# A decoder layer in fp32r products: eight plain half products for the first two MLP-down pairs, squares of x added on VectorE

## The chip, the cores and the metric

The kernel runs on one NeuronCore of a Trainium2 chip. The metric is the device time of one execution in microseconds (us). PE is TensorE (matmuls), DVE is VectorE, ACT is ScalarE, POOL is GpSimd and SP is SyncE, which issues DMAs.

## The reference, cut to what matters

One layer of a hybrid decoder on x of 512 tokens by 2048 features, all in float32. What the change touches are the sum of squares of the first norm, the norm of q and k, and the last product:

```python
def rms_norm(x, g):
    y = xf * lax.rsqrt(jnp.mean(xf * xf, axis=-1, keepdims=True) + EPS)
    return (y * g.astype(jnp.float32)).astype(x.dtype)
...
        xn = rms_norm(x, norm_mix_g[l])
        proj = xn @ w_in[l]
...
    q = rms_norm(q.reshape(b, s, ATTN_HEADS, HEAD_DIM), q_g)
    k = rms_norm(k.reshape(b, s, ATTN_HEADS, HEAD_DIM), k_g)
...
        x = x + merged @ w_out[l]
        h = rms_norm(x, norm_mlp_g[l]) @ w_mlp_up[l]
        x = x + jnp.square(jax.nn.relu(h)) @ w_mlp_down[l]
```

The hidden width of the MLP is 8192; attention has 8 heads of 64.

## The kernel before

Everything is held transposed: features on the 128 partitions, the 512 tokens along the free axis. A float32 product is made of three fp32r matmuls (`mm3`, L173): each factor is split into a rounded high part, cast on ACT, and a low part, the difference, made on DVE; hi x hi, hi x lo and lo x hi are added in PSUM. Names end in h and l for the parts (`x4h`, `x4l`, `wh`, `wl`).

**Front** (L245 to L266). A loop over the 16 feature tiles of x loads a tile, splits it with the norm's weight (`split`: ACT L221, DVE L222), splits the weights that belong to it (`fill`, L150 and L151, four k at a time), and multiplies it into `pq` and `pk`, the first q and k projection. ACT squares each tile (L227) and POOL adds it to `acc` (L229). Then `pv`, the values, begins with a weight piece of 1040 columns. `token_scale` turns `acc` into the norm's factor of each token while `pv` runs: its two PE steps come after the waits (3, 6). For ACT and DVE the instruction order of this part is set by the language's scheduler, for PE by the code.

**Chains.** Norms and attention run as generators that yield a time: `clock` adds up PE time by a formula as matmuls are issued, `poll` goes on with a chain whose time has come, and `finish` runs a chain to its end, setting the clock ahead where it must. `pair(i)` projects q and k of two heads (`proj`), normalises them (`qk_norm`: squares, `q3ms` on PE, a square root, a reciprocal, a split into `q3nh` and `q3nl`), and attends block by block: logits `pl`, softmax on DVE and ACT, transposition `pt` on PE, its copy `pT` on ACT (L472), and `po` on PE. Pairs 1 to 3 run beside the projections of the short convolutions (`pgc`, `pxx` and others).

**MLP.** From the gates on, PE, ACT and DVE follow one order written by the program. A product of a 256 x 256-block matrix by a matrix is done as seven products of halves instead of eight (Strassen's scheme in Winograd's form, products 1 to 7 in the order 1, 6, 7, 4, 5, 2, 3). That takes sums of quarters of the left factor (weights, `zd`, L671, made on DVE) and of the right (token sums, L858 to L861), and sums of the results (L933). An item is one or two left operands: DMA, sums, cast (L713), low part (L719); `step` prepares items two or three ahead of the one that PE multiplies, in left buffers of which there are three. What else DVE and ACT have to do waits in a list, `later`: `wait_for` puts a task in with a time, and a mark "must" for those that are taken at the next step whether or not there is room; `flush` takes tasks out by time alone until a right factor is there.

The right factors of MLP down are d0 to d38. Each is fetched by a POOL DMA (`std`, L909), cast (`shd`, L886) and made low (`sld`, L890), 1792 columns each. `h30` and `h31` are the last two outputs of MLP up: they are scaled (L1276), squared (L1284), get their token sums, and go to HBM, from where their factors are fetched again. The first two pairs of MLP down (`run_duo` with `down_first`) run together with K in two parts, so that they begin with d0 to d3 (part 0) and go on with d4 to d8 (part 1); seven PSUM banks hold both pairs. From pair 2 on, `run_pair` has eight factors a pair, into `pda` to `pdd`.

These lines put the factors of part 1 in the list and start the duo:

```python
    TIMES = (0, 2.5, 11, 13)
...
    renew((4, 5, 6, 7), TIMES, (6, 7, 8, 9))
    run_duo(
        down_first,
```

Of the kernel before, what the change touches and what calls it, by code (L numbers as in the profile page):

```python
# [11 lines left out]
ALU = mybir.AluOpType  # L12
# [86 lines left out]
def body(nc, tc, ctx, dram):  # L99
# [97 lines left out]
    def chain(steps):  # L197
        c = [steps, None]
        chains.append(c)
        advance(c)  # L200
        return c
# [23 lines left out]
    def add_square(acc, src, tag, name, eng):  # L225
        sq = acc if name.endswith("_0") else t512(tag, f"sq{name}")
        A.activation(sq, src, AF.Square)  # L227
        if sq is not acc:
            eng.tensor_tensor(out=acc, in0=acc, in1=sq, op=ALU.add)  # L229
# [12 lines left out]

    xg = []  # L245
    acc = t512("y", "acc1")
    pq, pk = bank("pq0", "aux"), bank("pk0", "aux")
    w0 = {}
    for k in range(KT):
        h, r = divmod(k, 8)  # L250
        if r == 0:
            w0 = {c: load(2 * h + e) for e, c in enumerate((XQ, XK))}
        raw = t512("m", f"xr{k}")
        for c in (XQ, XK):
            if r % 4 == 0:
                fill(*w0[c], slice(r * P, (r + 4) * P))
            if c == XQ and k == 0:
                nc.sync.dma_start(gm, dram["par"][:, :KT])
            if c == XQ:
                nc.sync.dma_start(raw, dram["xT"][k])  # L260
        xg.append(split(raw, "a", f"x{k}", gm[:, k : k + 1]))
        for c, ps in ((XQ, pq), (XK, pk)):
            mm3(ps, [p[:, r * P : (r + 1) * P] for p in w0[c][1:3]], xg[k], k == 0, k == KT - 1)
        add_square(acc, raw, "y", f"1_{k}", G)

    used[0] = len(weights)  # L266

    ident = const("ident", [P, P])
    rcnt = const("rcnt", [P, 16])
# [78 lines left out]
    def qk_norm(src, g, name):  # L348
        sq = t512("y", f"{name}sq")
        A.activation(sq, src, AF.Square)  # L350
        hi, lo = split(sq, "y", f"{name}q")
        yield 10
        ms = bank(f"{name}ms", "aux")
        mm(ms, eblk, hi, True, False)
        mm(ms, eblk, lo, False, True)
        v, s = t512("y", f"{name}v"), t512("y", f"{name}s")
        V.tensor_scalar(v, ms, EPS, None, ALU.add)
        inv_sqrt(sq, v, v, s)
        V.scalar_tensor_tensor(out=src, in0=src, scalar=g, in1=sq, op0=ALU.mult, op1=ALU.mult)
        qk[name] = split(src, "m", f"{name}n")  # L360

    def log1p_exp_neg_abs(z, mk, name):
# [33 lines left out]
    ncd = hbm.tile([8, S], F32, name="ncd")  # L396

    def first_pair():
        yield from token_scale(acc, "r1", n1)
        first.extend((proj(XQ, "q0", pq), proj(XK, "k0", pk)))  # L400

    def forget(z):
# [80 lines left out]

    def pair(i):
        q = proj(XQ + i * P, f"q{i}")
        qc = chain(qk_norm(q, qg8, f"q{i}"))
        k = proj(XK + i * P, f"k{i}")
        finish(qc)

        def steps():  # L490
            yield from qk_norm(k, pc("kg"), f"k{i}")
            yield 12
            yield from attend(i)

        chain(steps())
# [121 lines left out]
    class Phase:  # L617

        def __init__(self, kind, a, b, ks):
            self.kind, self.a, self.b, self.ks = kind, a, b, ks
            self.w = len(ks) * P
            self.raws, self.sums = {}, {}

# [8 lines left out]
        def quarter(self, q):  # L634
# [18 lines left out]
            o = 512 * (q % 2) if two else 0  # L653
            return self.raws[key][:, o : o + self.w]

        def room(self, n):

            two = self.w <= 512
            if n == 1 or not two:
                self.z = lz[0][1].tile([P, 1024], F32, name=f"z{self.kind}{self.a}_{n}", tag="z", bufs=2)  # L660
            o = 512 * (n - 1) if two else 0
            return self.z[:, o : o + self.w]

        def sums_of(self, i):
# [12 lines left out]

            def s2():
                x = a11()
                sums[2] = self.room(2)  # L680
                tt(sums[2], sums[1], x, ALU.subtract)

            return {
                1: [s1], 6: [s2], 7: [lambda: tt(a21(), a11(), a21(), ALU.subtract)],
                3: [lambda: tt(sums[2], a12(), sums[2], ALU.subtract)],
            }.get(i, [])

        def source(self, i):
            if i in (5, 6, 3):
                return self.sums[1 if i == 5 else 2]  # L690
            return self.quarter({1: 0, 7: 1, 4: 2, 2: 3}[i])

        def groups(self):
            return ((1, 6), (7, 4), (5, 2), (3,)) if self.w <= 512 else tuple((i,) for i in ORDER)

    class Item:
# [9 lines left out]
        def cast(self):  # L706
            self.hi, self.lo = (
                pool.tile([P, 1024], F32R, name=f"u{q}{self.name}", tag=f"w{q}", bufs=3) for q in "hl"
            )
            self.left = {}  # L710
            for n, i in enumerate(self.group):
                sl = slice(512 * n, 512 * n + self.phase.w)
                A.copy(self.hi[:, sl], self.phase.source(i))  # L713
                self.left[i] = (self.hi[:, sl], self.lo[:, sl])

        def sub(self):
            for i, (hi, lo) in self.left.items():
                spend(self.phase.w)
                V.tensor_tensor(out=lo, in0=self.phase.source(i), in1=f(hi), op=ALU.subtract)  # L719
# [73 lines left out]
    def flush(until=lambda: False):  # L793
        settle()
        while later and not until():
            pop(min(later, key=lambda t: t[0]))

    def result(name, where, tag, cols):

# [31 lines left out]
    def window(n, m):  # L831

        return [(J % UP, ("d", J)) for J in range(n, m)]

    def duo(kind, pairs, parts):

        return [[planned(Phase(kind, *pair, part)) for pair, part in zip(pairs, ps)] for ps in parts]

    def whole(kind, a, b, ks):
        return planned(Phase(kind, a, b, ks))  # L840
# [7 lines left out]
    up_first = duo("u", [(0, 0), (1, 0)], [[eight("u")[:4]] * 2, [eight("u")[4:]] * 2])  # L848
    up_pairs = [whole("u", n, 0, eight("u")) for n in range(2, UP - 2)]
    up_last = duo("u", [(UP - 2, 0), (UP - 1, 0)], [[eight("u")[:4]] * 2, [eight("u")[4:]] * 2])  # L850
    down_first = duo("d", [(0, 0), (1, 0)], [[window(0, 4), window(1, 4)], [window(4, 8), window(4, 9)]])
    down_pairs = [whole("d", n, 0, window(n, n + 8)) for n in range(2, UP)]

    def token_sums(t):
# [60 lines left out]
    def half_wide(name, where):  # L915
        return wide(name, where, "u", 1, S)

    def product(phase, i, left, ps, first, last, more):

        for n, (_, key) in enumerate(phase.ks):  # L920
            if key not in right:
                flush(lambda: key in right)
            wk = [t[:, n * P : (n + 1) * P] for t in left[i]]
            xk = [t[:, AT[i] * H : (AT[i] + 1) * H] for t in right[key]]
            mm3(ps, wk, xk, first and n == 0, last and n == len(phase.ks) - 1, more)
            poll()

# [3 lines left out]
    def add(out, ps, x):  # L931
        spend(H)
        V.tensor_tensor(out=out, in0=ps, in1=x, op=ALU.add)  # L933

    turn = [0]

# [240 lines left out]
    def residual(n, ps):  # L1177

        j, e = n % 8, n // 8
        r = t512("r", f"x1_{n}")  # L1180
        G.dma_start(r, dram["xT"][n])

        def first():
            spend(S)
            add_in(r, ps, r)
            G.dma_start(x1d[j][:, e * S : (e + 1) * S], r)
            wait_for(scaled, S, 0, n == 15)
            wait_for(square)

        def square():  # L1190
            sq = acc if n == 0 else t512("g", f"sq{n}")
            A.activation(sq, r, AF.Square)
            if n:
                wait_for(lambda: add_in(acc, acc, sq), S)

        def scaled():
            if e == 0:
                factors[j] = wide(f"x2_{j}", *((st1, "st1", 1) if j % 2 else (opool, "o", 1)))
            o = factors[j]
            V.scalar_tensor_tensor(  # L1200
                out=o[:, e * S : (e + 1) * S], in0=r, scalar=pc("g_mlp", n), in1=p, op0=ALU.mult, op1=ALU.mult,
            )
# [12 lines left out]

        return [first]
# [106 lines left out]
    def put(n, r):  # L1323
# [4 lines left out]
                nc.sync.dma_start(dram["out"][q + 8 * e], x1d[q][:, e * S : (e + 1) * S])  # L1328

    renew((4, 5, 6, 7), TIMES, (6, 7, 8, 9))  # L1330
    run_duo(
        down_first,
        [lambda n=n: (result(f"y{n}", upool[0], "o", 7 * H)[:, R], half_wide(f"ud{n}", upool[0])) for n in range(2)],
        lambda: renew((8, 9), (1, 9), (10, UP + 7)),
# [105 lines left out]
```

## Time and profile before

| | |
|---|---|
| time, 3 runs | 2760.41, 2760.54 (median), 2760.94 us |
| the profiled execution | 2758.59 us; its span 2756.7, mean granted clock 0.995 |
| PE busy | 2709.0 us, 98% of the span, 19904 matmuls |
| DVE busy | 2163.2 us, 78% |
| ACT busy | 1229.9 us, 45% |
| POOL busy | 180.8 us, 7% |

The profile is of one execution. Its span runs from the first instruction to the last; 1.89 us of the execution's time lie around it. A row's start is in us from the span's start. In a timeline, "[3.39 <-DVE x4l L222]" says that the engine was idle for 3.39 us before the row and that the write of `x4l` on DVE ended that. The start-to-start time of two instructions can be shorter than the duration shown, because they overlap in an engine's pipeline. The granted clock is a share of the full 2.4 GHz.

### The profile page before, as it was taken

The numbers are of one execution on the slowest core, as the hardware profiler recorded it, in microseconds if no ns is written. First come the engines' busy times: TensorE is split into PE (matmuls) and PEld (weight loads), VectorE is DVE, ScalarE is ACT, GpSimd is POOL, SyncE is SP. The second block draws the span as 40 slices with busy tenths as digits, with TensorE's granted clock in tenths as the row PEclk, the third lists the DMA queues.
The fourth block names the chain that finished last, engine by engine and source line by source line (L and its number), as shares of the span: only waits on it lengthen the run. The fifth ranks groups of instructions, "written<-read, shape, count | busy, mean of one in ns | idle before, by whom it ended". The sixth has DMA issues, their size and how long they took to land. (4 is left out here: it accounts for less than half of the span.)

```text
span 2756.7 us, 48177 instructions
## 1 busy us (share of the span) xinstructions
PE 2709.0 (98%) x19904; PEld 2540.5 (92%) x19904; DVE 2163.2 (78%) x2664; ACT 1229.9 (45%) x1520; POOL 180.8 (7%) x298
## 2 busy tenths in 40 slices
PE   8999999999999999999998999999997999999999
PEld 7787777789999999998888999999997999999999
DVE  6875655476889888887548988888888888888887
ACT  5443334454444444443224444444444544444443
POOL 3000000000000000003110000000000000000000
PEclk9999999999999999999999999999999999999999
DMA  5222223564444444447453444544446666656575
GB/s 178 94 98 80 84 77 103 182 229 161 143 158 141 139 145 156 143 146 252 144 177 120 174 165 144 164 144 165 144 146 210 185 186 173 189 170 190 170 206 155
DMA packets 143901, 429.49 MB, mean 156 GB/s; under 512 B 16696, under 2 KB 30904, under 8 KB 143680
## 3 DMA queue, kind: packets, MB, share of 16 engines
q1 hardware_dynamic: 101536, 279.19, 30.0%
q0 software_dynamic: 32496, 129.65, 16.2%
q10 hardware_dynamic: 9648, 17.57, 1.7%
q8 instruction: 156, 2.56, 0.4%
q14 instruction: 65, 0.53, 0.1%
HBM read 350.04 MB, written 79.97 MB: 156 GB/s over the span
## 5 line engine op out<-in xcount | busy, mean ns | idle before, releaser
L713 ACT CAST uhd<-wqd 128x1024 fp32r<-128x1024 f32 (+3 forms) x136 | 135.6, 999 | 216.8 <-PE pdd L173 80.8
L713 ACT CAST uhg<-wqg 128x1024 fp32r<-128x1024 f32 (+1 forms) x136 | 135.6, 999 | 185.3 <-PE pgd L173 96.4
L713 ACT CAST uhu<-wqu 128x1024 fp32r<-128x1024 f32 (+1 forms) x144 | 136.2, 951 | 159.8 <-PE pud L173 86.7
L719 DVE TENSOR_TENSOR uld<-wqd,uhd 128x1024 fp32r<-128x1024 f32 (+3 forms) x136 | 157.1, 1158 | 55.0 <-ACT uhd L713 55.0
L151 DVE TENSOR_TENSOR wl<-wr,wh 128x1024 fp32r<-128x1024 f32 (+2 forms) x100 | 121.6, 1218 | 90.1 <-ACT wh L150 86.1
L719 DVE TENSOR_TENSOR ulg<-wqg,uhg 128x1024 fp32r<-128x1024 f32 (+1 forms) x136 | 157.1, 1158 | 33.5 <-ACT uhg L713 33.5
L150 ACT CAST wh<-wr 128x1024 fp32r<-128x1024 f32 (+2 forms) x100 | 101.1, 1014 | 159.9 <-PE pb L173 32.2
L713 ACT CAST uhg<-zg 128x1024 fp32r<-128x1024 f32 (+1 forms) x102 | 102.0, 1000 | 150.0 <-DVE ulg L719 103.3
L719 DVE TENSOR_TENSOR ulu<-wqu,uhu 128x1024 fp32r<-128x1024 f32 (+1 forms) x144 | 157.7, 1100 | 7.4 <-ACT uhu L713 7.3
L713 ACT CAST uhu<-zu 128x1024 fp32r<-128x1024 f32 (+1 forms) x108 | 103.1, 955 | 125.3 <-DVE ulu L719 70.7
L713 ACT CAST uhd<-zd 128x1024 fp32r<-128x1024 f32 (+3 forms) x102 | 102.0, 1000 | 125.3 <-PE pdb L173 55.7
L173 PE MATMUL pda<-shd,uld 128*128 128x256 f32 x480 | 134.8, 281 | 1.1 <-DVE uld L719 1.1
L173 PE MATMUL pda<-sld,uhd 128*128 128x256 f32 x480 | 134.5, 280 | 0.0
L173 PE MATMUL pda<-shd,uhd 128*128 128x256 f32 x480 | 134.5, 280 | 0.0
L173 PE MATMUL pdd<-shd,uld 128*128 128x256 f32 x480 | 134.5, 280 | 0.0
L173 PE MATMUL pdb<-shd,uld 128*128 128x256 f32 x480 | 134.5, 280 | 0.0
L173 PE MATMUL pdb<-shd,uhd 128*128 128x256 f32 x480 | 134.5, 280 | 0.0
L173 PE MATMUL pdd<-shd,uhd 128*128 128x256 f32 x480 | 134.4, 280 | 0.0
L173 PE MATMUL pdd<-sld,uhd 128*128 128x256 f32 x480 | 134.4, 280 | 0.0
L173 PE MATMUL pdb<-sld,uhd 128*128 128x256 f32 x480 | 134.4, 280 | 0.0
L173 PE MATMUL pgb<-shg,ulg 128*128 128x256 f32 x480 | 134.2, 280 | 0.0
L173 PE MATMUL pgd<-shg,ulg 128*128 128x256 f32 x480 | 134.2, 280 | 0.0
(1462 smaller groups left out, 10455.2 us busy)
## 6 DMA issues: line engine op xcount, KB each, us to landing
wqg<-in_w SPq DMA_DIRECT2D x120, 512.0 KB, 3.5
wqu<-in_w SPq DMA_DIRECT2D x112, 512.0 KB, 3.5
wr<-in_w SPq DMA_DIRECT2D x84, 512.0 KB, 3.5
std<-zd POOLq DMA_DIRECT2D x39, 896.0 KB, 5.0
zd<-h POOLq DMA_DIRECT2D x32, 896.0 KB, 4.8
bk<-b ACTq DMA_DIRECT2D x64, 256.0 KB, 2.6
b<-bk POOLq DMA_DIRECT2D x32, 512.0 KB, 4.6
wo<-in_w SPq DMA_DIRECT2D x32, 512.0 KB, 3.6
```

The source lines that it names most:

```text
L150: A.copy(hi, raw)
L151: V.tensor_tensor(out=lo, in0=raw, in1=f(hi), op=ALU.subtract)
L173: T.matmul(out, w, x, start=start, stop=stop, skip_group_check=more)
L713: A.copy(self.hi[:, sl], self.phase.source(i))
L719: V.tensor_tensor(out=lo, in0=self.phase.source(i), in1=f(hi), op=ALU.subtract)
```

## The change

Six edits. (1) The squares of x are added on DVE; the additions are written behind the loop and the scheduler places them. (2) `first_pair` waits (10, 6) instead of (3, 6) in `token_scale`. (3) `qk_norm` yields 5 more before the split, and `pair` no longer finishes q's chain before it goes on. (4) The first two pairs of MLP down are eight plain products of halves: each quarter of the weights times its half of the tokens, no left sums; p0 and p1 hold the parts that are added into both rows, q and r the others, six PSUM banks in all. The first quarters are cast two at a time, 1024 wide. (5) `flush` takes tasks marked "must" first. (6) Among the residuals of the layer's first half, the scaling of both n = 7 and n = 15 is marked "must".

```diff
-        add_square(acc, raw, "y", f"1_{k}", G)
+        raws.append(raw)

     used[0] = len(weights)
+    for k, raw in enumerate(raws):
+        add_square(acc, raw, "y", f"1_{k}", V)
...
         V.scalar_tensor_tensor(out=src, in0=src, scalar=g, in1=sq, op0=ALU.mult, op1=ALU.mult)
+        yield 5
         qk[name] = split(src, "m", f"{name}n")
...
-        yield from token_scale(acc, "r1", n1)
+        yield from token_scale(acc, "r1", n1, (10, 6))
...
         q = proj(XQ + i * P, f"q{i}")
-        qc = chain(qk_norm(q, qg8, f"q{i}"))
+        chain(qk_norm(q, qg8, f"q{i}"))
         k = proj(XK + i * P, f"k{i}")
-        finish(qc)
...
         def groups(self):
+            if self.plain:
+                return ((0, 1), (2, 3)) if self.w <= 512 else ((0,), (1,), (2,), (3,))
...
         while later and not until():
-            pop(min(later, key=lambda t: t[0]))
+            pop(min(later, key=lambda t: (not t[4], t[0])))
...
+    PLAIN = {0: (("p0", 1), ("r0", 5)), 1: (("p1", 1), ("r1", 5)), 2: (("q1", 2), ("r1", 3)), 3: (("q0", 2), ("r0", 3))}
+
+    def run_plain_duo(phases, outs, between, after):
...
+                def products(item):
+                    then = []
+                    for i in item.group:
+                        for b, at in PLAIN[i]:
+                            p = ps[b][:, x * H : (x + 1) * H]
+                            opens = part == 0 and x == 0 and (b[0] != "r" or i < 2)
+                            closes = part == 1 and x == 1 and (b[0] != "r" or i > 1)
+                            product(phase, i, item.left, p, opens, closes, True, at)
+                            if part == 0 or b[0] == "r" and i < 2:
+                                continue
+                            if b[0] == "p":
+                                then.append(lambda p=p, u=(u2, u3)[i]: A.copy(u, p))
+                            else:
+                                c = {"q0": c11, "r0": c12, "q1": c21, "r1": c22}[b]
+                                then.append(lambda c=c, p=p, u=(u2, u3)[int(b[1])]: add(c, p, u))
+                    return then
...
-            wait_for(scaled, S, 0, n == 15)
+            wait_for(scaled, S, 0, j == 7)
...
     renew((4, 5, 6, 7), TIMES, (6, 7, 8, 9))
-    run_duo(
+    run_plain_duo(
         down_first,
```

Three places show the new orders. The first is DVE at the end of the front. The last `wl` of 1040 columns here belongs to the values `pv`; `eblk` is a constant. Before:

```order
L222 SCALAR_TENSOR_TENSOR x12l<-xr_295,gm,x12h 128x512
L346 TENSOR_SCALAR qg_372<-par 128x1
L518 TENSOR_SCALAR sp_689<-par 128x4
L222 SCALAR_TENSOR_TENSOR x13l<-xr_316,gm,x13h 128x512
L222 SCALAR_TENSOR_TENSOR x14l<-xr_331,gm,x14h 128x512
L276 MEMSET eblkf 128x128
L222 SCALAR_TENSOR_TENSOR x15l<-xr_346,gm,x15h 128x512
L278 MEMSET eblkf 64x64 x2
L279 CAST eblk<-eblkf 128x128
L151 TENSOR_TENSOR wl_386<-wr_384,wh_385 128x1040
L368 TENSOR_SCALAR lama<-lama 128x4
```

After:

```order
L229 TENSOR_TENSOR acc_83<-acc_83,sq_10_343 128x512
L278 MEMSET eblkf 128x128
L229 TENSOR_TENSOR acc_83<-acc_83,sq_11_346 128x512
L280 MEMSET eblkf 64x64
L229 TENSOR_TENSOR acc_83<-acc_83,sq_12_349 128x512
L280 MEMSET eblkf 64x64
L229 TENSOR_TENSOR acc_83<-acc_83,sq_13_352 128x512
L281 CAST eblk<-eblkf 128x128
L229 TENSOR_TENSOR acc_83<-acc_83,sq_14_355 128x512
L348 TENSOR_SCALAR qg_372<-par 128x1
L151 TENSOR_TENSOR wl_386<-wr_384,wh_385 128x1040
L229 TENSOR_TENSOR acc_83<-acc_83,sq_15_358 128x512
```

The additions stand between the low parts of x and ahead of `wl_386`; one, of tile 15, stands behind it.

The second is ACT at pair 3 of attention (`l,st` is the softmax, `wh` weights of the gates, `yd` the output of attention). Before:

```order
L288 ACT_TABLE_LOAD
L288 ACTIVATE q3s<-q3v 128x512
L150 CAST wh_3224<-wr_3223 128x1024
L350 ACTIVATE k3sq<-k_3214 128x512
L218 CAST k3qh<-k3sq 128x512
L150 CAST wh_3273<-wr_3272 128x1024
L218 CAST q3nh<-q_3098 128x512
L472 COPY pT_3255<-pt_3252 128x256
L482 COPY yd_2846<-po_3184 128x128
L453 ACT_TABLE_LOAD
```

After:

```order
L456 ACT_TABLE_LOAD
L456 ACTIVATE l_3186,st_3191<-l_3186,st_3191 128x384
L475 COPY pT_3199<-pt_3196 128x256
L150 CAST wh_3217<-wr_3216 128x1024
L352 ACTIVATE k3sq<-k_3207 128x512
L218 CAST k3qh<-k3sq 128x512
L150 CAST wh_3254<-wr_3253 128x1024
L218 CAST q3nh<-q_3068 128x512
L475 COPY pT_3288<-pt_3285 128x256
L456 ACTIVATE l_3275,st_3280<-l_3275,st_3280 128x384
L150 CAST wh_3320<-wr_3319 128x1024
```

`q3nh` still stands right ahead of a `pT`; a softmax block and another `pT` now stand between the square root of q (`q3s`) and `q3nh`.

The third is the beginning of MLP down: DVE around `sld` of d6 and d7, then ACT around `shd` of the same factors (`h_21287` is h30, `h_21425` is h31). DVE before; `sld` of d6 stands six rows above this piece:

```order
L861 TENSOR_TENSOR h_21287<-h_21287 128x256
L671 TENSOR_TENSOR zd_1_21737<-wqd_0_2_21734,zd_1_21737 128x512
L719 TENSOR_TENSOR uld_5_21817<-zd_1_21737,uhd_5_21816 128x512
L719 TENSOR_TENSOR uld_5_21817<-wqd_0_2_21734,uhd_5_21816 128x512
L1276 SCALAR_TENSOR_TENSOR h_21425<-h_21425,ups 128x512 x2
L858 TENSOR_TENSOR h_21425<-h_21425 128x256
L859 TENSOR_TENSOR h_21425<-h_21425 128x256
L860 TENSOR_TENSOR h_21425<-h_21425 128x256
L861 TENSOR_TENSOR h_21425<-h_21425 128x256
L890 TENSOR_TENSOR sld_21795<-std_21655,shd_21794 128x1792
```

DVE after; both low parts, of d6 and d7, are at its end:

```order
L1338 SCALAR_TENSOR_TENSOR h_21425<-h_21425,ups 128x512
L741 TENSOR_TENSOR uld_2_21632<-wqd_0_2_21633,uhd_2_21631 128x384 x2
L912 TENSOR_TENSOR sld_21642<-std_21474,shd_21641 128x1792
L1338 SCALAR_TENSOR_TENSOR h_21425<-h_21425,ups 128x512
L737 TENSOR_TENSOR uld_0_21696<-wqd_0_0_21697,uhd_0_21695 128x1024
L737 TENSOR_TENSOR uld_2_21743<-wqd_0_2_21744,uhd_2_21742 128x1024
L880 TENSOR_TENSOR h_21425<-h_21425 128x256
L881 TENSOR_TENSOR h_21425<-h_21425 128x256
L882 TENSOR_TENSOR h_21425<-h_21425 128x256
L883 TENSOR_TENSOR h_21425<-h_21425 128x256
L912 TENSOR_TENSOR sld_21749<-std_21639,shd_21748 128x1792
L912 TENSOR_TENSOR sld_21752<-std_21702,shd_21751 128x1792
```

ACT before:

```order
L713 CAST uhd_1_21759<-wqd_0_1_21731 128x512
L713 CAST uhd_1_21759<-zd_1_21737 128x512
L886 CAST shd_21763<-std_21611 128x1792
L713 CAST uhd_7_21787<-wqd_0_1_21731 128x512
L713 CAST uhd_7_21787<-wqd_0_2_21734 128x512
L886 CAST shd_21794<-std_21655 128x1792
L1284 ACTIVATE h_21287<-h_21287 128x1024
L713 CAST uhd_5_21816<-zd_1_21737 128x512
L713 CAST uhd_5_21816<-wqd_0_2_21734 128x512
L1284 ACTIVATE h_21425<-h_21425 128x1024
```

ACT after:

```order
L725 CAST uhd_0_21695<-wqd_0_0_21697 128x1024
L725 CAST uhd_2_21742<-wqd_0_2_21744 128x1024
L908 CAST shd_21748<-std_21639 128x1792
L908 CAST shd_21751<-std_21702 128x1792
L1346 ACTIVATE h_21425<-h_21425 128x1024
L731 CAST uhd_0_21799<-wqd_0_0_21801 128x640
L731 CAST uhd_1_21860<-wqd_0_1_21862 128x640
```

On DVE the left sums are gone and the token sums of h31 stand ahead of both low parts instead of between them; on ACT the square of h31 stands behind both casts, with the two casts of part 1's first left operands ahead of them.

## Rows read from the trace of the kernel before

**Rows 1.** The page: busy time and share of the span of each engine, and instructions.

```profile
PE 2709.0 (98%) x19904; PEld 2540.5 (92%) x19904; DVE 2163.2 (78%) x2664; ACT 1229.9 (45%) x1520; POOL 180.8 (7%) x298
```

**Rows 2.** The waits of PE, grouped by who waits for what: total us, times, longest.

```profile
PE pd L173 <- DVE sld L890: 11.1, 2, 10.3
PE pu L173 <- DVE ulu L719: 9.9, 5, 4.0
...
PE po L173 <- ACT pT L472: 4.6, 2, 3.5
PE pq L173 <- DVE x4l L222: 3.4, 1, 3.4
PE pq L173 <- DVE x12l L222: 3.3, 1, 3.3
```

**Rows 3.** Busy time in stretches of the span: stretch, its length, then busy us (and instructions) of PE, weight loads, DVE, ACT and POOL, the granted clock of PE, the busy share of the DMA engines, GB/s. The first three lie in the front, the fourth behind the wait for `pT` at pair 3, the last two at the beginning of MLP down.

```profile
8.30:21.40 13.10, 9.71 (x33) 7.37 (x33) 12.71 (x9) 10.01 (x18) 12.55 (x8) 0.87 1.06 393
21.50:24.30 2.80, 2.80 (x14) 2.25 (x13) 2.80 (x5) 1.27 (x3) 0.00 (x0) 1.00 0.39 158
24.40:35.90 11.50, 8.19 (x31) 6.21 (x31) 11.19 (x10) 10.38 (x19) 11.03 (x7) 0.90 0.31 93
...
409.40:415.80 6.40, 6.34 (x17) 4.87 (x18) 1.62 (x4) 2.26 (x5) 0.03 (x1) 0.50 0.01 4
...
2132.90:2136.30 3.40, 3.33 (x16) 3.34 (x17) 0.01 (x1) 0.10 (x1) 0.53 (x1) 0.52 0.93 316
...
2140.00:2158.00 18.00, 16.69 (x136) 15.91 (x134) 16.65 (x24) 7.22 (x10) 1.42 (x2) 1.00 0.68 198
```

**Rows 4.** The timeline of POOL in the front: start, busy us, instruction, count.

```profile
8.28 13.16 POOL L229 TENSOR_TENSOR acc<-acc,sq 128x512 f32<-128x512 f32 x8 [7.83 <-ACT sq L227]
24.33 11.62 POOL L229 TENSOR_TENSOR acc<-acc,sq 128x512 f32<-128x512 f32 x7 [2.89 <-ACT sq L227]
```

**Rows 5.** The timeline of DVE in the front.

```profile
7.71 0.75 DVE L222 SCALAR_TENSOR_TENSOR x1l<-xr,gm,x1h 128x512 fp32r<-128x512 f32 x1
...
15.17 1.76 DVE L222 SCALAR_TENSOR_TENSOR x4l<-xr,gm,x4h 128x512 fp32r<-128x512 f32 x1
...
22.52 0.74 DVE L222 SCALAR_TENSOR_TENSOR x8l<-xr,gm,x8h 128x512 fp32r<-128x512 f32 x1
23.18 0.74 DVE L222 SCALAR_TENSOR_TENSOR x9l<-xr,gm,x9h 128x512 fp32r<-128x512 f32 x1
```

**Rows 6.** The timeline of PE in the front.

```profile
13.20 0.39 PE L173 MATMUL pq<-x4h,wh 128*128 128x512 f32 x1
...
20.96 0.39 PE L173 MATMUL pq<-x6h,wh 128*128 128x512 f32 x1
...
29.36 0.39 PE L173 MATMUL pq<-x12h,wh 128*128 128x512 f32 x1
...
40.16 0.28 PE L173 MATMUL pv<-wl,x0h 128*128 128x260 f32 x1
```

**Rows 7.** The timelines of PE and ACT at pair 3 of attention, and of ACT at pair 2.

```profile
395.01 0.50 PE L173 MATMUL q3ms<-q3qh,eblk 128*128 128x512 f32 x1
...
408.51 0.62 ACT L218 CAST q3nh<-q 128x512 fp32r<-128x512 f32 x1 [3.14 <-DVE q L359]
409.04 0.37 ACT L472 COPY pT<-pt 128x256 f32<-128x256 f32 x1
...
409.46 1.12 PE L173 MATMUL po<-pT,val 128*64 128x128 f32 x4 [3.54 <-ACT pT L472]
...
335.18 0.62 ACT L218 CAST q2nh<-q 128x512 fp32r<-128x512 f32 x1 [2.22 <-DVE q L359]
336.26 0.37 ACT L472 COPY pT<-pt 128x256 f32<-128x256 f32 x1 [0.46 <-PE pt L179]
```

**Rows 8.** The timelines of PE and, for the last two rows, of ACT at the beginning of MLP down.

```profile
2100.88 0.41 PE L173 MATMUL pd<-shd,uhd 128*128 128x256 f32 x1
...
2118.06 0.28 PE L173 MATMUL pd<-shd,uld 128*128 128x256 f32 x1
...
2120.04 0.28 PE L173 MATMUL pd<-sld,uhd 128*128 128x256 f32 x1
...
2132.97 0.58 PE L173 MATMUL pd<-sld,uhd 128*128 128x256 f32 x1 [10.28 <-DVE sld L890]
...
2158.93 0.39 PE L173 MATMUL pda<-shd,uld 128*128 128x256 f32 x1 [0.91 <-DVE uld L719]
...
2120.57 1.68 ACT L886 CAST shd<-std 128x1792 fp32r<-128x1792 f32 x1
...
2128.09 1.06 ACT L1284 ACTIVATE h<-h 128x1024 f32<-128x1024 f32 x1 [3.85 <-DVE h L1276]
```

**Rows 9.** The timeline of DVE at the beginning of MLP down.

```profile
2096.51 0.68 DVE L671 TENSOR_TENSOR zd<-wqd,wqd 128x512 f32<-128x512 f32 x1
2097.23 0.69 DVE L671 TENSOR_TENSOR zd<-zd,wqd 128x512 f32<-128x512 f32 x1
2097.84 0.68 DVE L719 TENSOR_TENSOR ulu<-zu,uhu 128x512 fp32r<-128x512 f32 x1
...
2129.18 0.42 DVE L858 TENSOR_TENSOR h<-h 128x256 f32<-128x256 f32 x1 [1.12 <-ACT h L1284]
...
2130.89 2.02 DVE L890 TENSOR_TENSOR sld<-std,shd 128x1792 fp32r<-128x1792 f32 x1
```

More of the change, by code (lines that the diff above doesn't have):

```diff
@@ L241, in pc @@
         return par[:rows, c : c + 1]
-    xg = []
+    xg, raws = [], []
     acc = t512("y", "acc1")
@@ L617, in body, with __init__ @@
     class Phase:
-        def __init__(self, kind, a, b, ks):
-            self.kind, self.a, self.b, self.ks = kind, a, b, ks
+        def __init__(self, kind, a, b, ks, plain=False):
+            self.kind, self.a, self.b, self.ks, self.plain = kind, a, b, ks, plain
             self.w = len(ks) * P
@@ L654, in quarter, with raw @@
             return self.raws[key][:, o : o + self.w]
+        def raw(self, q):
+            self.quarter(q)
+            return self.raws[q // 2]
         def room(self, n):
@@ L664, in sums_of @@
         def sums_of(self, i):
+            if self.plain:
+                return []
             a11, a21, a22, a12 = (lambda q=q: self.quarter(q) for q in range(4))
@@ L688, in source @@
         def source(self, i):
+            if self.plain:
+                return self.quarter(i)
             if i in (5, 6, 3):
@@ L693, in groups @@
         def groups(self):
+            if self.plain:
+                return ((0, 1), (2, 3)) if self.w <= 512 else ((0,), (1,), (2,), (3,))
             return ((1, 6), (7, 4), (5, 2), (3,)) if self.w <= 512 else tuple((i,) for i in ORDER)
@@ L710, in cast @@
             self.left = {}
+            if self.phase.plain and self.phase.w == 512:
+                A.copy(self.hi, self.phase.raw(self.group[0]))
+                for n, i in enumerate(self.group):
+                    self.left[i] = [t[:, 512 * n : 512 * (n + 1)] for t in (self.hi, self.lo)]
+                return
             for n, i in enumerate(self.group):
@@ L716, in sub @@
         def sub(self):
+            if self.phase.plain and self.phase.w == 512:
+                spend(1024)
+                V.tensor_tensor(out=self.lo, in0=self.phase.raw(self.group[0]), in1=f(self.hi), op=ALU.subtract)
+                return
             for i, (hi, lo) in self.left.items():
@@ L833, in window, with duo @@
         return [(J % UP, ("d", J)) for J in range(n, m)]
-    def duo(kind, pairs, parts):
-        return [[planned(Phase(kind, *pair, part)) for pair, part in zip(pairs, ps)] for ps in parts]
+    def duo(kind, pairs, parts, plain=False):
+        return [[planned(Phase(kind, *pair, part, plain)) for pair, part in zip(pairs, ps)] for ps in parts]
     def whole(kind, a, b, ks):
@@ L850, in body @@
     up_last = duo("u", [(UP - 2, 0), (UP - 1, 0)], [[eight("u")[:4]] * 2, [eight("u")[4:]] * 2])
[L851 removed]
+    down_first = duo("d", [(0, 0), (1, 0)], [[window(0, 4), window(1, 4)], [window(4, 8), window(4, 9)]], True)
     down_pairs = [whole("d", n, 0, window(n, n + 8)) for n in range(2, UP)]
@@ L916, in half_wide, with product @@
         return wide(name, where, "u", 1, S)
-    def product(phase, i, left, ps, first, last, more):
+    def product(phase, i, left, ps, first, last, more, at=None):
         for n, (_, key) in enumerate(phase.ks):
@@ L923, in product @@
             wk = [t[:, n * P : (n + 1) * P] for t in left[i]]
-            xk = [t[:, AT[i] * H : (AT[i] + 1) * H] for t in right[key]]
+            c = AT[i if at is None else at] * H
+            xk = [t[:, c : c + H] for t in right[key]]
             mm3(ps, wk, xk, first and n == 0, last and n == len(phase.ks) - 1, more)
@@ L933, in add @@
         V.tensor_tensor(out=out, in0=ps, in1=x, op=ALU.add)
+    PLAIN = {0: (("p0", 1), ("r0", 5)), 1: (("p1", 1), ("r1", 5)), 2: (("q1", 2), ("r1", 3)), 3: (("q0", 2), ("r0", 3))}
+    def run_plain_duo(phases, outs, between, after):
+        turn[0] += 2
+        sums = ("p0", "r0", "p1", "r1", "q1", "q0")
+        ps = {i: bank(f"p{phases[0][0].kind}{i}", "mm" if n < 4 else "aux") for n, i in enumerate(sums)}
+        for part in range(2):
+            if part:
+                between()
+            for x in range(2):
+                phase = phases[part][x]
+                if part:
+                    out, u = outs[x]()
+                    c11, c12, c21, c22, u2, u3 = blocks(out, u)
+                def products(item):
[14 more added lines that the diff above has]
+                    return then
+                for _ in phase.groups():
+                    step(products)
+                if part:
+                    after[x](out)
     turn = [0]
```

## Prediction

> **What bounds the kernel now.** I read the engine totals first. TensorE (PE) is busy 98% of the span, the next engine 78% [rows 1], so time leaves only where PE waits, where it runs at its lower clock, or where its instructions are fewer. Next the waits of PE [rows 2]: five groups hold most of its idle time. Two, `pq` for `x4l` (3.4 us) and for `x12l` (3.3), lie in the front; `po` for `pT` (4.6, longest 3.5) in attention; `pu` for `ulu` (9.9, longest 4.0) and `pd` for `sld` (11.1, longest 10.3) where MLP up turns into MLP down. A long wait also costs afterwards: right behind these waits the granted clock is 0.50 to 0.52, that is 1.2 GHz, for 3 to 6 us, while it is 1.00 elsewhere, also over 18 us near the end of the first two down pairs in which PE idles 1.31 us in short waits (16.69 busy of 18.00) [rows 3].
>
> **Front.** In the loop over the 16 tiles of x, POOL adds the squares: 8 adds in 13.16 us and 7 in 11.62, 1.65 us each [rows 4]. While it does, one x-low of VectorE (DVE) takes 1.76 us; before POOL starts and in the pause between the two runs it takes 0.74 to 0.75 [rows 5]. The DMA share doesn't go with it: it is 1.06 in the first run, but 0.31 in the second, where x-lows are as slow, and 0.39 in the pause [rows 3]. So I take POOL's adds as the cause.
>
> The change takes the 15 adds from POOL and gives DVE 15 of 128x512. Their price beside a quiet POOL is not in this trace; the bounds are 0.60 us (about the start-to-start time from `zd` to `ulu`, both of 512 columns, 2097.23 to 2097.84 [rows 9]) and 1.76 (the slow x-low). I take 0.60, since that is a DVE add with POOL not adding, and for x-lows 0.66 (22.52 to 23.18 [rows 5]). Walking DVE and ACT in the new order with these, `x4l` is ready at about 12.2 and `x12l` at 22.9. PE, no longer stopped, takes 8.40/6 = 1.40 us for one k (six tiles from 20.96 to 29.36 [rows 6]) and comes to them at 13.4 and 24.6. Both waits go, and the slow clock behind them. The loop, from 13.20 on, ends at 13.20 + 12 x 1.40 = 30.0.
>
> What is late next is the first low weight for the values, `wl` of 1040 columns: it stands behind `x15l` and five of the adds, starts at 30.15 and ends at 31.4. PE's second `pv` matmul, at 40.16 now [rows 6], then comes at 31.4, after a wait of 1.3 us: **-8.75 us**. Were the adds 0.1 us dearer, the fourteen ahead of `wl` would give back 1.4.
>
> [...]
>
> Waits (10, 6) instead of (3, 6) for the token scale let PE work on for 7 us before the ones matmuls want the accumulator; the last add ends at about 32, early enough. I count 0.
>
> **Attention.** At pair 3, ACT casts `q3nh` at 408.51, when `q` is ready at last, and copies `pT` only behind it; PE waits 3.54 us for that and then runs at the low clock [rows 7]. The granted clock is 0.50 from there to 415.8 [rows 3], and half of the 5 us of 512-column matmuls in it, 2.5, is lost: this stall costs 3.54 + 2.5 = 6.0. The order on ACT stays, `q3nh` and then `pT` (ACT rows of the change's section); what moves is PE. The finish that is dropped had set the planner's clock ahead of PE's work, so that `po` came early in PE's order: it is wanted 10.9 us after `q3ms` (395.01 to 405.9) and `pT` ready 14.4 after [rows 7]. In the new order 17.7 us of PE's work lie between, and by my walk of DVE and ACT `pT` is ready 14.6 after `q3ms`. That wait goes, with 3 us to spare. At pair 2, `q2nh` stands ahead of a `pT` in both orders, at 335.18 and 336.26 now, without a wait of PE [rows 7]; in the new order it is an earlier `pT`, which PE wants 1.2 us before it is there, too short for the clock. Sum **-4.8**, bounds -6.0 (no new wait) and 0 (the stall moves to pair 2 at its old price).
>
> **The first two pairs of MLP down.** Eight products of halves instead of seven: 16 factors x 8 x 3 = 384 matmuls of 256 columns, not 336. At the full clock they start 0.117 us apart (17 steps from 2118.06 to 2120.04 [rows 8]), so 48 x 0.117 = **+5.6** on PE, the busy engine. In return DVE loses all left sums (four a phase, 16 in all; the two of 512 columns shown start 0.72 and 0.61 before what follows [rows 9], so about 10 us), and its casts, subtractions and result adds are fewer.
>
> What that is worth lies in one wait. `sld7` starts at 2130.89 and PE resumes at 2132.97 [rows 8, 9]; it stands on DVE behind the left sums, the scaling and squaring of h31 and the token sums of h31 (2129.18). The new order, by the same durations: before the transition, `h30` scaled (0.6) takes the place of two left sums (1.3) ahead of `ulu`, so PE starts down at 2100.15 instead of 2100.88. Part 0 is then 168 matmuls, 19.7 us and 0.6 at the low clock: 2120.5; the six of part 1 that have their factors bring it to 2121.2. On ACT the second cast of part 1 waits for a left buffer that PE frees after 132 matmuls, at 2116.3; behind it stand `shd6`, `shd7` (1.69 long) and the squaring of h31 (1.06) [rows 8], which ends at 2121.7. DVE's token sums of h31 follow, 2121.7 to 2123.5, then `sld6` to 2125.5 and `sld7` (2.02 long) to 2127.45. So PE waits 4.2 and 1.3 us and resumes at 2127.47, 5.5 us earlier than now, with 206 matmuls of the first two pairs left instead of 179.
>
> I compare at the third matmul of pair 2, at 2158.93 after a wait of 0.91 [rows 8]. From the resumption to it are 181 matmuls and 25.96 us: 21.2 of matmuls, 1.31 of short waits for left factors, 0.91, 1.63 for the low clock (0.48 of 3.40 [rows 3]) and 0.9 that I can't place. In the new order the left factors stand ahead of the result adds, so the short waits and the 0.91 go: 208 x 0.117 + 1.63 + 0.9 = 26.9, at 2154.4. **-4.6**. Bounds: -10.28 - 1.63 - 1.31 - 0.91 + 5.6 = -8.5 (every wait gone), and +5.6 (nothing gained).
>
> "Must first" in flush, and the last residual of up scaled at j = 7: at most one 512-column add in another place, 0.6; I take 0.
>
> **Sum.** -8.75 - 4.8 - 4.6 = -18.15. On the profiled execution (2758.59) this gives 2740.4. The runs shown have a median 1.95 above that execution, so I say **2742**.
>
> **Rivals.**
> (a) The transition gives nothing: the wait at `sld7` keeps its 10 us because ACT's chain (buffer, `shd7`, square) or the transfer of d7 comes later than I walked. For it: five ACT steps hang on one freed buffer, and the new left casts are 1024 wide. Against: DVE loses some 10 us of work there. Then -13.5 + 0 to +5.6: 2747 to 2753. Chance 0.17.
> (b) The front gives back part: `wl` comes later, because an add costs a full 0.69 or waits for its square on ACT. For it: 1.3 us of wait is already forecast, the chain of adds is dependent, and dependent sums start 0.72 apart (2096.51 to 2097.23 [rows 9]). 15 x 0.1 to 0.2 = 1.5 to 3: 2744 to 2745. Chance 0.12. It lies in the forecast's own range.
> (c) Attention's stall only moves to pair 2, and the transition gives nothing: -8.75 + 5.6 = -3.2: 2757, no change. Chance 0.04.
> (d) Slower: the slow x-lows are not POOL's doing but that of ACT's traffic in the same stretch (ACT is busy 10.0 of the 13.1 us [rows 3]). Then the 14 adds ahead of `wl` cost 1.7 each on a DVE that is already full: 23.5 us later there, with the 8.75 not gained, +23.5 - 4.8 - 4.6 = +14: 2775. It decides from 9.4/14 = 0.7 us per add on. Against: in the pause of POOL, with ACT still busy 1.27 of 2.80 us, the x-low falls at once to 0.74 [rows 3, 5]. Chance 0.04.
> (e) More than forecast, both late waits gone: 2733 to 2737. Chance 0.08.
> Forecast itself: 0.55, its own range 2737 to 2747.
>
> **Numbers.** The range 2733 to 2753 takes in (a), (b) and (e) nearly whole; outside are (c), (d) and what I have not seen, some 0.15. No change, within 0.2%, is 2755.0 to 2766.1 (0.2% is 5.5 us, about what a measurement of this kernel can tell). Faster: 0.55 + 0.17 + 0.12 + 0.08 = 0.92; same 0.04; slower 0.04.
>
> **What will show it.** Front: x-lows all near 0.75 us, no PE wait for `x4l` or `x12l`, `pv` at about 31 with a wait of 1 us for `wl`. If x-lows stay at 1.76, (d) holds. Attention: no wait of over 3 us for `pT`, clock 1.00 where it was 0.50. Transition: h31's token sums ahead of both `sld6` and `sld7`, PE's longest `pd` wait about 4 us, with a second of 1.3, and the third matmul of pair 2 at 2154.4 - 13.55 = 2140.8. A longest wait of over 8 us means (a).

## The result and the profile after

The changed kernel takes 2745.34 us (median of 4 runs, 2743.41 to 2747.65) where the kernel before takes 2760.74 (4 runs, 2760.41 to 2761.14): a ratio of 0.9945, with a 95% interval of 0.993 to 0.996. The forecast was 2742, in a range of 2733 to 2753. The direction and the range held; the gain is 15.4 us where 18.2 to 18.7 were forecast, and it is made up otherwise than I said.

The profiled execution took 2745.49 us, its span is 2743.7 against 2756.7. Its waits of PE, which answer to [rows 2] (who waits for what, total us, times, longest):

```profile
PE pu L173 <- DVE ulu L741: 9.7, 6, 3.3
PE pq L173 <- ACT x0h L221: 6.8, 1, 6.8
PE pdp L173 <- DVE sld L912: 5.0, 2, 3.9
PE pb L173 <- DVE y10l L219: 1.3, 1, 1.3
PE po L173 <- ACT pT L475: 1.2, 2, 1.0
PE pv L173 <- DVE wl L151: 1.2, 1, 1.2
PE pb L173 <- ACT y10h L218: 1.1, 1, 1.1
```

The waits for `x4l`, for `x12l` and the long one for `pT` are gone, and that for `sld` fell from 11.1 to 5.0. New are 1.2 us for `wl`, which was forecast, and two waits of `pb` for `y10`, the first factor of the second branch, which were not. The very first wait, for the first tile of x, is 6.8 us long instead of 5.4: its DMA landed later, and the code up to it is the same.

The front on DVE, to be held against [rows 5] (timeline: start, us, instruction):

```profile
12.28 0.74 DVE L222 SCALAR_TENSOR_TENSOR x4l<-xr,gm,x4h 128x512 fp32r<-128x512 f32 x1
...
23.70 0.74 DVE L222 SCALAR_TENSOR_TENSOR x12l<-xr,gm,x12h 128x512 fp32r<-128x512 f32 x1
24.37 0.68 DVE L229 TENSOR_TENSOR acc<-acc,sq 128x512 f32<-128x512 f32 x1
24.97 0.75 DVE L222 SCALAR_TENSOR_TENSOR x13l<-xr,gm,x13h 128x512 fp32r<-128x512 f32 x1
...
31.98 1.23 DVE L151 TENSOR_TENSOR wl<-wr,wh 128x1040 fp32r<-128x1040 f32 x1
```

and on PE, against [rows 6]:

```profile
6.84 0.79 PE L173 MATMUL pq<-x0h,wh 128*128 128x512 f32 x1 [6.84 <-ACT x0h L221]
...
33.27 0.39 PE L173 MATMUL pv<-wl,x0h 128*128 128x260 f32 x1 [1.17 <-DVE wl L151]
```

All x-lows take 0.74 to 0.75 us, an addition starts 0.60 before what follows (24.37 to 24.97), and from PE's first matmul to the second of `pv` it is 33.27 - 6.84 = 26.43 us, where it was 40.16 - 5.39 = 34.77.

The beginning of MLP down, against [rows 8, 9]. DVE, then ACT, then PE:

```profile
2113.95 0.42 DVE L880 TENSOR_TENSOR h<-h 128x256 f32<-128x256 f32 x1 [2.91 <-ACT h L1346]
...
2115.68 3.95 DVE L912 TENSOR_TENSOR sld<-std,shd 128x1792 fp32r<-128x1792 f32 x2
...
2109.69 3.27 ACT L908 CAST shd<-std 128x1792 fp32r<-128x1792 f32 x2
2112.87 1.05 ACT L1346 ACTIVATE h<-h 128x1024 f32<-128x1024 f32 x1
...
2117.75 0.44 PE L173 MATMUL pdp<-sld,uhd 128*128 128x256 f32 x1 [3.88 <-DVE sld L912]
2119.68 0.58 PE L173 MATMUL pdp<-sld,uhd 128*128 128x256 f32 x1 [1.07 <-DVE sld L912]
...
2146.50 0.28 PE L173 MATMUL pda<-shd,uld 128*128 128x256 f32 x1
```

DVE waits 2.91 us for the square of h31, then does its token sums and then both low parts back to back; that is the order forecast, and PE's two waits for it are 3.88 and 1.07 long (4.2 and 1.3 forecast).

Where the time went, read at four PE instructions that both traces have: at the second `pv` matmul the changed kernel is 6.89 us ahead (40.16 to 33.27), 8.34 of it from the loop, less 1.45 for the later first tile. At a matmul late in MLP up it is 7.76 ahead (2085.92 to 2078.16), so attention and all that follows it have brought 0.9. At the third matmul of pair 2 of MLP down it is 12.43 ahead (2158.93 to 2146.50): 4.67 from the transition. At the end of the span it is 13.0.

### The profile page after: what moved, and what is told of

Read it like the earlier page. It is cut to its first block, busy times and chain, and to the rows that moved or that the text cites. A ratio compares the mean times of both kernels' runs of the same rounds, so it can differ in the third digit from the quotient of the medians.

```text
span 2743.7 us, 48190 instructions
## 1 busy us (share of the span) xinstructions
PE 2711.5 (99%) x19952; PEld 2544.5 (93%) x19952; DVE 2137.7 (78%) x2641; ACT 1223.0 (45%) x1506; POOL 156.5 (6%) x283
## 5 line engine op out<-in xcount | busy, mean ns | idle before, releaser
L731 ACT CAST uhd<-wqd 128x1024 fp32r<-128x1024 f32 (+2 forms) x128 | 130.8, 1024 | 230.3 <-PE pdd L173 86.8
L741 DVE TENSOR_TENSOR uld<-wqd,uhd 128x1024 fp32r<-128x1024 f32 (+2 forms) x128 | 151.8, 1187 | 69.6 <-ACT uhd L731 69.6
L731 ACT CAST uhd<-zd 128x1024 fp32r<-128x1024 f32 x90 | 94.5, 1050 | 105.7 <-PE pdb L173 55.7
```

## The experiments

**The lost gain of attention.** In the trace after, at the point where PE goes over to the second branch (PE, then ACT):

```profile
489.49 0.57 PE L173 MATMUL pb<-y10h,wh 128*128 128x512 f32 x1 [1.14 <-ACT y10h L218]
491.32 0.80 PE L173 MATMUL pb<-y10l,wh 128*128 128x512 f32 x1 [1.26 <-DVE y10l L219]
491.91 0.63 PE L173 MATMUL pb<-y10h,wl 128*128 128x512 f32 x1
492.34 0.63 PE L173 MATMUL pb<-y11h,wh 128*128 128x512 f32 x1
...
488.38 0.48 ACT L475 COPY pT<-pt 128x384 f32<-128x384 f32 x1
...
488.81 0.62 ACT L218 CAST y10h<-w 128x512 fp32r<-128x512 f32 x1
```

`y10h` stands on ACT behind a `pT` of the last pair, in both kernels. Before (ACT, then PE):

```profile
495.54 0.62 ACT L218 CAST y10h<-w 128x512 fp32r<-128x512 f32 x1
...
502.26 0.40 PE L173 MATMUL pb<-y10h,wh 128*128 128x512 f32 x1
```

Before, PE had 7 us of other products between that block's transposition and `y10`; now it has none. Behind the two waits matmuls of 512 columns start 0.43 us apart instead of 0.23. The rows say that this costs 2.4 us of waits and as much again at the low clock, which is about what the stall at pair 3 had cost. Two runs test it.

```diff
-            yk = ys[0] if k == 0 else [split(y, "y", f"y{k}{q}") for q, y in enumerate(ys[k])]
+            yk = ys[0] if k == 0 else [split(y, "m", f"y{k}{q}") for q, y in enumerate(ys[k])]
```

> The changed kernel, with the split parts of the second branch's factors (y10 to y13) in the buffers of the m group instead of the y group. Theory A: the gain at attention is lost at the first product of the second branch: with the added yield the attention chain runs some 7 us of PE time later, the softmax block l62 is read by its transposition right ahead of that product, and y10h takes a buffer that only comes free there. Then the two waits (1.14 and 1.26 us) go, and the 5 us at the low clock behind them (2.5 us): -4.9, 2740.4 us. Rival B: y10h is late because ACT has no room earlier; then the waits stay and the time is 2745.

Measured: 2740.67 us (2739.68 to 2743.63), ratio 0.9927 (0.9912 to 0.9942). The waits for `y10` are gone, and `y10h` is cast at 418.74, some 70 us earlier. The stretch from 480 to 500 us, in the changed kernel and then in this one (stretch, length, busy us of PE, weight loads, DVE, ACT and POOL, granted clock, DMA share, GB/s):

```profile
480.00:500.00 20.00, 17.60 (x67) 12.61 (x66) 6.76 (x10) 7.90 (x14) 1.22 (x1) 0.83 0.32 115
```

```profile
480.00:500.00 20.00, 20.00 (x89) 14.73 (x87) 5.67 (x7) 7.79 (x13) 1.22 (x1) 1.00 0.46 151
```

2.4 us of idle time and a clock of 0.83 have become 0 and 1.00: theory A holds. That a buffer of the y group was what held `y10h` is shown by this edit; that it is the one of the softmax block read last is argued from the order alone.

```diff
         V.scalar_tensor_tensor(out=src, in0=src, scalar=g, in1=sq, op0=ALU.mult, op1=ALU.mult)
-        yield 5
         qk[name] = split(src, "m", f"{name}n")
```

> The changed kernel without the added yield of 5 in the norm of q and k; the dropped finish stays dropped. Theory A: the yield alone moves the chain; without it PE's order is that of before, the wait for pT at pair 3 is back with 3.5 us and 2.5 us of low clock (+6.0), the waits for y10h and y10l and their low clock go (-4.9), as does 0.2 at pair 2: 2746.2 us. Rival B: dropping the finish is what moved PE's order, and the yield does nothing: 2745.3, with the wait for y10 still there.

Measured: 2746.08 us (2744.54 to 2747.52), ratio 0.9944 (0.993 to 0.9959). Its ACT and PE at pair 3 are those of [rows 7] again, 7.8 us earlier:

```profile
400.74 0.62 ACT L218 CAST q3nh<-q 128x512 fp32r<-128x512 f32 x1 [3.14 <-DVE q L361]
401.26 0.36 ACT L474 COPY pT<-pt 128x256 f32<-128x256 f32 x1
...
401.68 0.76 PE L173 MATMUL po<-pT,val 128*64 128x128 f32 x4 [3.54 <-ACT pT L474]
```

The stall is back, to the hundredth of a us, and the waits for `y10` are gone; from 60 to 1390 us the order of PE's instructions is that of the kernel before. So the dropped finish by itself moved nothing, and the yield moved PE's order. Whether the yield would do the same with the finish kept, no run shows. Its worth is 0.7 us by the medians, inside the intervals, because it traded one stall for another. The low clock behind the returned stall was shorter than before: 0.74 from 401.6 to 408.1 us, against 0.50 over as long [rows 3]. So the price of one and the same wait is not fixed.

**The front: the engine or the order.** The squares were moved in two respects: to DVE, and behind the loop, where the scheduler may order them anew. Two runs complete the table.

```diff
-        add_square(acc, raw, "y", f"1_{k}", V)
+        add_square(acc, raw, "y", f"1_{k}", G)
```

> The changed kernel with the 15 additions of squares given back to POOL, still written behind the loop. Theory A: a POOL addition slows every DVE operation beside it; x-lows take 1.76 us again beside POOL, PE waits some 3 us for an x-low once or twice and runs at the low clock behind it: +6 to +9, 2751 to 2754 us. Rival B: what helped was the order that the scheduler finds when the squares are written behind the loop; then DVE, relieved of 15 additions, has the x-lows early all the same: 2743 to 2746.

Measured: 2750.4 us (2748.32 to 2751.9), ratio 0.996 (0.9945 to 0.9975). DVE, then POOL:

```profile
12.29 0.68 DVE L151 TENSOR_TENSOR wl<-wr,wh 128x512 fp32r<-128x512 f32 x1
12.89 1.78 DVE L222 SCALAR_TENSOR_TENSOR x4l<-xr,gm,x4h 128x512 fp32r<-128x512 f32 x1
...
21.98 0.74 DVE L222 SCALAR_TENSOR_TENSOR x8l<-xr,gm,x8h 128x512 fp32r<-128x512 f32 x1
...
25.84 1.78 DVE L222 SCALAR_TENSOR_TENSOR x12l<-xr,gm,x12h 128x512 fp32r<-128x512 f32 x1
...
33.83 0.74 DVE L222 SCALAR_TENSOR_TENSOR x15l<-xr,gm,x15h 128x512 fp32r<-128x512 f32 x1
...
12.76 8.15 POOL L229 TENSOR_TENSOR acc<-acc,sq 128x512 f32<-128x512 f32 x5 [0.94 <-ACT sq L227]
25.62 13.84 POOL L229 TENSOR_TENSOR acc<-acc,sq 128x512 f32<-128x512 f32 x8 [4.71 <-ACT sq L227]
```

DVE's operations on 512 columns are 1.76 to 1.79 us long while POOL adds (12.76 to 20.91, and 25.62 to 32.7), and 0.68 to 0.74 in POOL's pauses, which now lie elsewhere than in [rows 4, 5]. `x15l` is the exception: 0.74 us beside a POOL addition. That settles whose doing it is, against rival (d). The size fell between the two theories, near A: PE's waits are six of 0.17 to 0.95 us, and the granted clock is 1.00 throughout the front. I put that down to the new order, in which two weight operations no longer stand together ahead of `x4l`; no run tests it.

```diff
-        raws.append(raw)
+        add_square(acc, raw, "y", f"1_{k}", V)
...
-    for k, raw in enumerate(raws):
-        add_square(acc, raw, "y", f"1_{k}", V)
```

> The changed kernel with the additions of the squares on DVE but written inside the loop, as they stood on POOL. Theory A: it is the engine that counts most: DVE's operations take 0.60 to 0.66 from start to start, the last weight for the values is ready at the same time, the low part of tile 12 comes at most 0.4 us late: 2745 to 2746 us. Rival B: the order found by the scheduler counts as much as the engine, as the run with the squares on POOL suggests (it got back half of the gain with POOL adding): 2748 to 2750.

Measured: 2745.06 us (2744.59 to 2745.24), ratio 0.9949 (0.9934 to 0.9963); PE waits 0.55 us for `x12l`, a little over the 0.4 expected. (This run, that of the small edits and the two with the sums of h31 moved shared runs of the kernel before with a median of 2758.66 us, 2.1 less than above; between the two sets I compare the gains on before.) The time fits theory A; the gain, 1.8 us below that of the changed kernel, lies between A and B, and the traces decide. The second `pv` matmul with the squares on POOL, then with them in the loop:

```profile
37.01 0.39 PE L173 MATMUL pv<-wl,x0h 128*128 128x260 f32 x1 [0.83 <-DVE wl L151]
```

```profile
33.50 0.39 PE L173 MATMUL pv<-wl,x0h 128*128 128x260 f32 x1 [0.62 <-DVE wl L151]
```

From PE's first matmul (6.37 and 5.60 there) to this one, in us:

| | inside the loop | behind it |
|---|---|---|
| on POOL | 34.77 (before) | 37.01 - 6.37 = 30.64 |
| on DVE | 33.50 - 5.60 = 27.90 | 26.43 (after) |

Either edit alone brings 4.1 (order) or 6.9 (engine), both 8.3, so the engine counts most, as A said, and the order is no small part. With the engine changed, the order is worth 1.5 in the front; the gains, 13.6 and 15.4 us, have intervals that overlap.

**Eight products or seven.** The duo of before with all else as changed:

```diff
-    run_plain_duo(
+    run_duo(
         down_first,
```

> The changed kernel with the first two pairs of MLP down as seven products again; flush still takes must tasks first. Theory A: the eight products pay because the left sums keep DVE from the low parts of d6 and d7; 48 matmuls fewer give 5.6 us back, the long wait for the low part of d7 costs about 10: +4.7, 2750 us. Rival B: the order of flush alone brings the low parts forward; then seven products are the better choice, 2740 us.

Measured: 2753.02 us (2750.61 to 2753.61), ratio 0.997 (0.9957 to 0.9982): 7.7 slower than the changed kernel, where theory A said 4.7. The size has another cause than A's. PE's waits in this stretch:

```profile
PE pd L173 <- DVE sld L912: 7.0, 2, 6.2
...
PE pd L173 <- DVE uld L741: 3.3, 4, 1.8
PE pda L173 <- DVE uld L741: 2.1, 3, 0.8
...
PE pd L173 <- ACT uhd L731: 1.1, 1, 1.1
```

and DVE's two low parts and the token sums of h31:

```profile
2110.83 2.02 DVE L912 TENSOR_TENSOR sld<-std,shd 128x1792 fp32r<-128x1792 f32 x1
...
2117.95 2.02 DVE L912 TENSOR_TENSOR sld<-std,shd 128x1792 fp32r<-128x1792 f32 x1
...
2135.03 0.43 DVE L880 TENSOR_TENSOR h<-h 128x256 f32<-128x256 f32 x1 [1.12 <-ACT h L1346]
```

With must tasks first, flush does bring `sld7` ahead of h31's sums, and the wait for it is 6.2 instead of 10.3 us; but DVE's load is the same, and it falls due in part 1 as waits for left factors. In that stretch, 2120 to 2152, PE's clock is 0.84. From the last `ulu` to the third matmul of pair 2 DVE is busy 52.9 of 61.7 us here (52.8 of 60.4 before), and 36.1 of 56.3 with eight products. So the place of one instruction is not what pays. That the smaller load on DVE is, I read from these waits and sums; the eight products also changed the casts and the banks, and no run parts them.

**The small edits.** Token scale waits, flush, and the one must mark taken back:

```diff
-        yield from token_scale(acc, "r1", n1, (10, 6))
+        yield from token_scale(acc, "r1", n1, (3, 6))
...
-            pop(min(later, key=lambda t: (not t[4], t[0])))
+            pop(min(later, key=lambda t: t[0]))
...
-            wait_for(scaled, S, 0, j == 7)
+            wait_for(scaled, S, 0, n == 15)
```

> The changed kernel with three small edits taken back: token scale waits (3, 6), flush by time alone, must for the scaling of n = 15 only. All theories: each is worth at most 0.6 us; 2744.5 to 2746.5 us. If the token scale's earlier matmul waits for the last square, up to 1 us shows as a wait of PE ahead of the ones matmuls.

Measured: 2745.25 us (2741.82 to 2746.24), ratio 0.9947 (0.9932 to 0.9962). The gain on before is 13.4 us, and 15.4 with the three edits; the intervals of the ratios overlap almost wholly. Together they are worth nothing that can be told here (2 us could hide in the intervals), and no wait ahead of the ones matmuls appears.

**What is left in the transition.** After, the token sums of h31 stand ahead of two low parts that PE waits for, while nobody soon needs those sums. The edit puts them back in the list:

```diff
-        wait_for(sums, 4 * 300)
+        wait_for(sums, 4 * 300, 18 if n == UP - 1 else 0)
```

> The changed kernel with the token sums of h31 behind the low parts of d6 and d7, and nothing else. Theory A: -5.9 against 2745.3, that is 2739.4 us, with a single wait of about 1.2 us for a low part at the second half of the first down pairs. Rival B: 2744.5 to 2745.5.

Measured: 2738.16 us (2736.46 to 2739.95), ratio 0.9926 (0.9909 to 0.9943). The gain on before is 20.5 us where the changed kernel has 15.4: 5.1 for the edit, of the 5.9 that theory A said (7.2 by the medians as they stand). The wait that remains is 1.22 us long, as said. So the sums of h31, which wait for its square, were what held up the low parts; with the sums out of the way, DVE waits only 0.37 us for `shd` before both low parts. Both edits together:

> The changed kernel with y10 to y13 in the m buffers and, besides, the token sums of h31 put back by 18 us in the list, so that on DVE they stand behind the low parts of d6 and d7. Theory A: the wait for the low part of d6 (3.88 us) is that for the token sums of h31, which wait for its square on ACT behind both casts; with the low parts first, d6 is ready at 2113.4 in the time of the changed kernel, wanted at 2113.9, and d7 at 2115.4 against 2119.7 now: -4.3, and no low clock behind, -1.6. With y1 (-4.9) the time is 2740.7 - 5.9 = 2734.8 us. Rival B: the casts on ACT set the end and not DVE; then the gain is under 1 us: 2740.

Measured: 2732.4 us (2732.19 to 2734.2), ratio 0.9904 (0.989 to 0.9919). The gain on before is 26.3 us, about the sum of its parts (15.4, 4.7 and 5.1); it beats both kernels. Its waits of PE, and DVE at d6 and d7:

```profile
PE pu L173 <- DVE ulu L741: 8.3, 6, 1.9
PE pq L173 <- ACT x0h L221: 5.9, 1, 5.9
PE pv L173 <- DVE wl L151: 1.3, 1, 1.3
PE pdp L173 <- DVE sld L912: 1.2, 1, 1.2
```

```profile
2104.53 3.96 DVE L912 TENSOR_TENSOR sld<-std,shd 128x1792 fp32r<-128x1792 f32 x2 [0.37 <-ACT shd L908]
...
2109.14 0.42 DVE L880 TENSOR_TENSOR h<-h 128x256 f32<-128x256 f32 x1
```

But for the first tile of x, no wait is left that is longer than 1.9 us; the sums of h31 come 1 us after the low parts and hold up nothing.

## Why the prediction was right, and where it was not

**Front: right, -8.75 said, -8.34 measured** from PE's first matmul on. Both waits and their low clock went, x-lows fell to 0.75, and a wait of 1.17 us for `wl` came (1.3 said). The price of 0.60 for an addition was right: one of 0.68 us at 24.37 is followed at 24.97. The Trainium skill, page "VectorE: DVE Perf Modes", section "The DRAIN you can't avoid", has the next operation wait until the pipe is empty, but adds that one which is not held starts earlier. The trace agrees with this addition. The cause, POOL, was right, and the squares on POOL show it. What I did not see is that the order alone would have got half of it. The trace's net at this point is only 6.89, because the first tile landed 1.45 us later. In the ten executions profiled PE's first matmul starts between 5.39 (before) and 6.84 (after), with the same code ahead of it.

**Token scale and the small edits: right as far as can be told**, 0 said; taken back together they change the gain by 2.0 us, within the intervals.

**Attention: the term that failed, -4.8 said, at most -0.9 measured** (up to late in MLP up). The stall at pair 3 did go, and pair 2's new wait is 0.17 instead of 1.2. The failed step is "That wait goes, with 3 us to spare", followed by a sum that ended there. The chain's work did not vanish; PE did it later, up to the point where the second branch begins, and there `y10h` was behind it. The prediction asked what is late next inside attention and did not walk on to the chain's last block. The runs show the price: 4.7 us by the medians (2745.34 to 2740.67), against 6.0 for the stall in the one trace that I had; with the shorter low clock of the run without the yield the same stall costs less. My account of the cause was wrong as well: it named the dropped finish, which by itself moved nothing; the yield did.

**MLP down: right, -4.6 said, -4.67 measured.** The steps hold one by one. Shifted by the 7.76 us that the kernel is ahead there, the token sums of h31 were forecast at 2121.7 - 7.76 = 2113.94 and start at 2113.95; the resumption at 2127.47 - 7.76 = 2119.71, and it is 2119.68. Walking two engines by the order printed and by the durations of the trace was enough for this. The last stretch came out by luck as well: from the resumption to pair 2 I had 1.63 us for the low clock and 0.9 that I could not place; the low clock cost 2.4 (to 2124.75), and nothing is left over. Rival (a) fell.

**The sum.** 18.15 us less were forecast for the profiled execution, 13.1 came (2758.59 to 2745.49). Of the 5 us missing, 3.9 are attention, 1.45 the late first tile and 0.4 the front; another 0.6 was won behind pair 2's first product, which I can't place. By the medians, of several landings of that tile, 3 are missing, and the new stall of `y10` alone is larger than that. So the range held with one of three terms nearly gone; a total that fits is no test of each term.

## What to carry to other kernels

When a chain of small steps is put off, walk it to its last step and on to the first instruction that stands behind it in a buffer or a queue: a stall that is moved off one place may be waiting at the end of the chain. A sum of squares on POOL is not free beside DVE: read the length of the same DVE operation in POOL's pauses before counting POOL's work as hidden. And when an algorithm with fewer matmuls loads the engine that feeds PE, price it in the stage where that engine is late; here the scheme with 48 matmuls more (5.6 us) is 7.7 us faster with that price paid.

## What the runs showed of the hardware that I had not expected

Waits of 1 to 2 us lowered the clock in some places and not in others. After, 1.14 and 1.26 us with one matmul between them are followed by matmuls 0.43 us apart for 4.9 us (491.32 to 496.2), and in all six executions that have this pair of waits the clock fell during it or right behind it; behind the single wait of 1.17 us for `wl` in the same trace the clock is 1.00 from 33 to 45 us. But neither the length of a wait nor their number decides alone. A wait of 1.92 or 1.93 us for an `ulu`, some 14 us ahead of MLP down, is in all ten executions: in four the granted clock of the 9 us behind it is 0.81, in six it is 1.00. In those same four, waits of 1.8 to 1.9 and of 0.9 us follow, some 2.6 us apart, and the clock behind them is 1.00. I had counted waits of this length as too short for the clock, one by one.

A POOL addition stretches DVE's operations to nearly one length, whatever their form: 1.76 to 1.78 us for x-lows and for weight operations alike, of 0.68 to 0.75 without it. It is not so for every one: `x15l` with the squares on POOL takes 0.74 beside an addition, and `wl` of 1040 columns at 35.72 takes 1.23, as without POOL, beside the longest of the additions (2.30).

The length of a wait is not what it costs. The wait for `ulu` right ahead of MLP down was 1.8 to 1.9 us long in four of the executions and 3.2 to 4.1 in the six others; it differs even between two kernels that are the same up to there. After, then with h31's sums put back:

```profile
2078.16 0.39 PE L173 MATMUL pu<-shu,ulu 128*128 128x256 f32 x1 [1.93 <-DVE ulu L741]
...
2090.16 0.39 PE L173 MATMUL pu<-shu,ulu 128*128 128x256 f32 x1 [3.29 <-DVE ulu L741]
```

```profile
2076.25 0.38 PE L173 MATMUL pu<-shu,ulu 128*128 128x256 f32 x1 [1.92 <-DVE ulu L741]
...
2088.30 0.38 PE L173 MATMUL pu<-shu,ulu 128*128 128x256 f32 x1 [1.82 <-DVE ulu L741]
```

From one resumption to the next it is 12.00 and 12.05 us, so the shorter wait won nothing. The four executions with the short wait are those whose clock fell to 0.81 behind the wait before it: PE got there later, and DVE was ready when it would have been anyway. What single executions do differ by is the landing of the first tile (1.45 us) and how long the clock stays low behind the same stall; the medians say more than one profile does.
